# Summing rows of 1,024: each partition owns 113 consecutive rows, and the lead tile is no longer transposed

## The chip, the cores and the metric

The kernel runs on one core of one Trainium2 chip. The metric is the device time of one execution in microseconds (us).

## The reference

```python
batch, seq, dim = 32, 512, 1024
x = np.random.randn(batch, seq, dim).astype(np.float32)
multiplier = 0.5
out = (np.sum(x, axis=-1) * multiplier).astype(np.float32)
```

16,384 rows of 1,024 floats (67.1 MB) are read, and 16,384 floats (64 KB) are written.

## The kernel before

**Rows and partitions.** There are 128 partitions and 128 rows for each. The rows of x are cut into three regions, one after the other in DRAM:

- `x_rows`: the first 128 × 112 rows. Partition p owns the 112 consecutive rows from 112p on (`own = 112`), so neighbouring partitions are 112 × 4 KB = 448 KB apart.
- `x_last`: the next 128 × 15 rows (`tail = 15`), 15 consecutive rows (60 KB) for each partition.
- `x_lead`: the last 128 rows of x, one for each partition, a single stretch of 512 KB.

**Loads.** All DMAs are issued by SyncE (SP), through the helper `load` (line 83), which gives each a semaphore of its own. First comes the lead tile, then seven blocks of 16 rows per partition (8.39 MB each; 64 KB per partition in one piece) into three buffers `buf[0..2]` in turn. From the fourth block on a load waits until DVE has summed the block that held its buffer. `start_loads_at_entry` moves the lead load and the first three block loads, which wait for nothing, to the start of the program, ahead of the common preamble. The tail's 15 rows come last, in pieces of 7, 5 and 2 rows into a block buffer, and the last row cut into 608 and 416 columns into the tile `end`. Each such tile is 128 partitions wide.

**Sums.** DVE sums the lead tile with one `dve_sum` (lines 98 to 109: one instruction adds the two halves of a row and accumulates), while block 0 is still on its way. The result is 128 sums in one column, one in each partition. It goes to column 0 of a zeroed 32×32-block tile `lead_sq`, and a DVE transpose (line 129) turns it into `lead_tr`, where partitions 0, 32, 64 and 96 hold 32 sums each. These four partitions are stored with a DMA of their own (line 171, `lead_store`).

The blocks are summed by one `reduce_sum` per block (line 134) and multiplied into `res` (line 140). In the last block DVE does 8 rows and ACT the other 8 (`act_row`, line 90). In the tail the rows of the set `on_act` go to ACT, the others to DVE by `dve_sum`. The two pieces of the last row are summed by DVE in `first` and `final`, the second adding up both.

**Stores.** The early store (line 167) writes `res[:, 0:112]`, 448 bytes from each partition, once the last block is summed; the lead store follows it on the same queue. The last store (line 195) writes the tail's 15 columns, 60 bytes from each partition, after ACT's and DVE's last sums. Then SyncE waits for the three stores in the order early, lead, last (lines 199 to 201).

Of the kernel before, what the change touches and what calls it, by code (L numbers as in the profile page):

```python
# [9 lines left out]
def kernel(  # L10
# [13 lines left out]
    nc = tc.nc  # L24
# [4 lines left out]
    P = nc.NUM_PARTITIONS  # L29
# [3 lines left out]
    x_flat = x.flatten_outer_dims()  # L33
    N, D = x_flat.shape
    rows = N // P
    out_flat = out.rearrange("b s -> (b s)")
    mul = float(multiplier)

    B = 16
    n_blocks = rows // B  # L40
    assert N == P * rows and rows == n_blocks * B
    own = rows - B
    tail = B - 1
    lead0 = P * (own + tail)
    x_rows = x_flat[0 : P * own, :].rearrange("(p c) d -> p c d", p=P)
    x_last = x_flat[P * own : lead0, :].rearrange("(p c) d -> p c d", p=P)
    x_lead = x_flat[lead0:N, :]
    out_rows = out_flat[0 : P * own].rearrange("(p c) -> p c", p=P)
    out_last = out_flat[P * own : lead0].rearrange("(p c) -> p c", p=P)
    out_lead = out_flat[lead0:N].rearrange("(q c) -> q c", c=32)  # L50

    def sbuf(name, *shape):
        return ctx.enter_context(nc.sbuf_tensor(name, list(shape), fp32)).ap()
# [4 lines left out]
    res = sbuf("res", P, rows)  # L58
    cut = 608
    at = 640  # L60
    end = sbuf("end", P, at + D - cut)
    S = 32
    lead = sbuf("lead", P, D)
    lead_sq = sbuf("lead_sq", P, S)
    lead_tr = sbuf("lead_tr", P, S)

    def sem(name):
        return nc.alloc_semaphore(name=name)

    dve_done = sem("dve_done")  # L70
# [3 lines left out]
    def marks(i, engine):  # L74

        s = dve_done if engine == "dve" else act_done
        i.then_inc(s, 1)
        counts[engine] += 1
        return counts[engine]

    def load(name, dst, src, free=None):
        landed = sem(name)
        i = nc.sync.dma_start(out=dst, in_=src)  # L83
        if free is not None:
            i.wait_op(dve_done, free, "sem-ge")
        i.then_inc(landed, 16)
        return landed

    def act_row(t, r, col):
        return nc.scalar.activation(  # L90
            out=t[:, r, :],
            in_=t[:, r, :],
            func=mybir.ActivationFunctionType.Copy,
            scale=mul,
            accum_out=res[:, col : col + 1],
        )

    def dve_sum(row, dst, scale):
        mid = row.shape[-1] // 2
        return nc.vector.tensor_tensor_reduce(  # L100
            out=row[:, 0:mid],
            in0=row[:, 0:mid],
            in1=row[:, mid:],
            scale=scale,
            scalar=0.0,
            op0=ADD,
            op1=ADD,
            accum_out=dst,
        )

    marks(nc.vector.memset(end[:, at - 2 : at], 0.0), "dve")  # L111
    zeroed = marks(nc.vector.memset(lead_sq, 0.0), "dve")  # L112
    freed = []
    lead_landed = load("lead_landed", lead, x_lead)
    for b in range(n_blocks - 1):
        c0 = b * B
        t = buf[b % bufs]
        landed = load(
            f"landed{b}",
            t,  # L120
            x_rows[:, c0 : c0 + B, :],
            freed[b - bufs] if b >= bufs else None,
        )
        h = B if b < n_blocks - 2 else B // 2
        if b == 0:
            nc.vector.wait_ge(lead_landed, 16)
            nc.vector.wait_ge(dve_done, zeroed)
            summed = marks(dve_sum(lead, lead_sq[:, 0:1], mul), "dve")
            turned = nc.vector.transpose(out=lead_tr, in_=lead_sq)  # L129
            turned.wait_op(dve_done, summed, "sem-ge")  # L130
            marks(turned, "dve")
        nc.vector.wait_ge(landed, 16)
        done = marks(
            nc.vector.reduce_sum(  # L134
                out=sums[:, c0 : c0 + h], in_=t[:, 0:h, :], axis=mybir.AxisListType.X
            ),
            "dve",
        )
        freed.append(done)
        scaled = nc.vector.tensor_single_scalar(  # L140
            out=res[:, c0 : c0 + h],
            in_=sums[:, c0 : c0 + h],
            scalar=mul,
            op=mybir.AluOpType.mult,
        )
        scaled.wait_op(dve_done, done, "sem-ge")
        early_dve = marks(scaled, "dve")
        if h < B:
            nc.scalar.wait_ge(landed, 16)
            for r in range(h, B):  # L150
                i = act_row(t, r, c0 + r)
            early_act = marks(i, "act")

    c0 = (n_blocks - 1) * B
    t = buf[(n_blocks - 1) % bufs]
    nc.sync.wait_ge(dve_done, freed[n_blocks - 1 - bufs])
    pieces = [(0, 7), (7, 12), (12, 14)]
# [4 lines left out]
    landed_end = [  # L162
        load(f"landed_e{k}", end[:, to : to + hi - lo], x_last[:, tail - 1, lo:hi])
        for k, (to, lo, hi) in enumerate(((0, 0, cut), (at, cut, D)))
    ]
    nc.sync.wait_ge(dve_done, early_dve)
    early = nc.sync.dma_start(out=out_rows, in_=res[:, 0:own])
    early.wait_op(act_done, early_act, "sem-ge")
    early_stored = sem("early_stored")
    early.then_inc(early_stored, 16)  # L170
    lead_store = nc.sync.dma_start(out=out_lead, in_=lead_tr[0:P:S, :])
    lead_stored = sem("lead_stored")
    lead_store.then_inc(lead_stored, 16)

    on_act = {4, 5, 6, 10, 11, 13}
    for k, (lo, hi) in enumerate(pieces):
        on = [r for r in range(lo, hi) if r in on_act]
        nc.scalar.wait_ge(landed[k], 16)
        for r in on:
            i = act_row(t, r, c0 + r)  # L180
        late_act = marks(i, "act") if k == len(pieces) - 1 else None
        on = [r for r in range(lo, hi) if r not in on_act]
        nc.vector.wait_ge(landed[k], 16)
        for r in on:
            dve_sum(t[:, r, :], res[:, c0 + r : c0 + r + 1], mul)
    nc.vector.wait_ge(landed_end[0], 16)
    first = dve_sum(end[:, 0:cut], end[:, at - 1 : at], 1.0)

    first.then_inc(landed_end[1], 1)
    final = dve_sum(end[:, at - 2 :], res[:, rows - 2 : rows - 1], mul)  # L190
    final.wait_op(landed_end[1], 17, "sem-ge")
    done = marks(final, "dve")

    nc.sync.wait_ge(act_done, late_act)
    store = nc.sync.dma_start(out=out_last, in_=res[:, own : own + tail])
    store.wait_op(dve_done, done, "sem-ge")
    stored = sem("stored")
    store.then_inc(stored, 16)
    nc.sync.wait_ge(early_stored, 16)
    nc.sync.wait_ge(lead_stored, 16)  # L200
    nc.sync.wait_ge(stored, 16)

    def start_loads_at_entry(nc_):
# [61 lines left out]
```

## Time and profile before

| what | value |
|---|---|
| median of 3 runs | 160.57 us (160.52 to 160.6) |
| profiled execution, its own time | 160.62 us |
| its span, first to last instruction | 159.3 us |
| DVE busy | 120.2 us (75%) |
| ACT busy | 16.3 us (10%) |
| HBM read, written | 67.11 MB, 0.07 MB |
| mean DMA rate over the span | 422 GB/s |
| lead load, issue to landing | 3.2 us |
| early store, last store, issue to landing | 9.6 us, 1.4 us |

Times in the profile count from the first instruction of the span. A group of instructions is named by its line, engine, operation and tiles; L83 is line 83 of the kernel, where all loads are issued, and SPq is SyncE's instruction queue. In a timeline line the first number is the start, the second the duration, and the bracket the engine's idle time just before and what ended it. In a line of waits the numbers are the total, the count and the longest. The line of a DMA queue gives packets, MB and the packets' time as a share of sixteen DMA engines' span. TensorE is not used.

### The profile page before, as it was taken

Reading aid. Unit: us, or ns where it says so; the run is one execution under the profiler, and the core shown is the slowest. Engines: PE = TensorE matmul, PEld = TensorE weight load, DVE = VectorE, ACT = ScalarE, POOL = GpSimd, SP = SyncE. Lnnn points to the kernel's source line nnn. Section 1 sums busy time; section 2 is a strip of 40 time slices with the busy share of each in tenths; the row PEclk is TensorE's granted clock in tenths of the full one; section 3 lists DMA queues with packets and bytes.
Section 4 is the critical chain, followed back from the end, with each engine's and each line's share of the span. In section 5 each row is a group of like instructions: output and inputs, shape, how many; then the busy total and the mean of one; then the engine's idle time right before and its main releaser. Section 6 shows DMA issues by size and latency. Waiting matters only on the chain.

```text
span 159.3 us, 128 instructions
## 1 busy us (share of the span) xinstructions
DVE 120.2 (75%) x39; ACT 16.3 (10%) x29; POOL 0.2 (0%) x4
## 2 busy tenths in 40 slices
DVE  2000029999499995999869997899959999599744
ACT  2000000000000000000000000000000000099844
POOL 0000000000000000000000000000000000000000
DMA  9969989899699699699699898996996996999994
GB/s 395 510 280 527 411 379 527 379 411 527 263 527 527 263 527 527 263 527 494 296 527 428 362 527 379 411 527 280 510 527 263 527 527 263 436 403 433 442 397 144
DMA packets 2168, 67.18 MB, mean 422 GB/s; under 512 B 504, under 2 KB 632, under 8 KB 888
## 3 DMA queue, kind: packets, MB, share of 16 engines
q1 hardware_dynamic: 2168, 67.18, 98.0%
HBM read 67.11 MB, written 0.07 MB: 422 GB/s over the span
## 4 chain that ended last, share of the span: by engine, by line
DMA 75%; DVE 22%; SPq 1%; issue 0%
DMA xb<-in_x_dram 52%; DMA end<-in_x_dram 24%; DVE sums L134 22%; SPq L83 1%; DVE end L100 1%; DVE res L140 0%; DVE res L100 0%
## 5 line engine op out<-in xcount | busy, mean ns | idle before, releaser
L134 DVE TENSOR_REDUCE sums<-xb 128x16 f32<-128x16384 f32 (+1 forms) x7 | 112.0, 16001 | 30.3 <-DMA xb<-in_x_dram 30.3
L90 ACT ACTIVATE xb<-xb 128x1024 f32<-128x1024 f32 x14 | 14.6, 1046 | 138.1 <-DMA xb<-in_x_dram 138.0
L100 DVE CUSTOM_DVE_ANT_0 xb<-xb 128x512 f32<-128x512 f32 x8 | 5.1, 689 | 3.9 <-DMA xb<-in_x_dram 3.9
L90 ACT ACTIVATION_READ_ACCUMULATOR xb<-xb 128x1 f32 x14 | 2.6, 188 | 0.0
L111 DVE MEMSET end<- 128x2 f32 x1 | 0.1, 60 | 2.9 <-PEq L26 2.9
L90 ACT ACT_TABLE_LOAD x1 | 1.3, 1283 | 2.9 <-PEq L26 2.9
L140 DVE TENSOR_SCALAR res<-sums 128x16 f32<-128x16 f32 (+1 forms) x7 | 1.2, 174 | 0.2
L100 DVE CUSTOM_DVE_ANT_0 end<-end 128x304 f32<-128x304 f32 (+1 forms) x2 | 0.9, 428 | 0.1
L100 DVE CUSTOM_DVE_ANT_0 lead<-lead 128x512 f32<-128x512 f32 x1 | 0.7, 693 | 0.2 <-DMA lead<-in_x_dram 0.2
L100 DVE DVE_READ_ACCUMULATOR2_ANT res<- 128x1 f32 x9 | 0.8, 83 | 0.0
L129 DVE STREAM_TRANSPOSE lead_tr<-lead_sq 128x32 f32<-128x32 f32 x1 | 0.2, 211 | 0.0
L246 POOL MEMSET const-bfloat16-1.0<- 128x1 bf16 x1 | 0.1, 101 | 0.0
L246 POOL MEMSET const-uint8-127<- 128x1 uint8 x1 | 0.1, 101 | 0.0
L246 POOL MEMSET const-float32-0.0<- 128x1 f32 x1 | 0.1, 98 | 0.2 <-issue 0.2
L246 POOL MEMSET const-float32-1.0<- 128x1 f32 x1 | 0.1, 98 | 0.0
L112 DVE MEMSET lead_sq<- 128x32 f32 x1 | 0.1, 85 | 0.0
L100 DVE DVE_READ_ACCUMULATOR2_ANT end<- 128x1 f32 x1 | 0.1, 84 | 0.0
L100 DVE DVE_READ_ACCUMULATOR2_ANT lead_sq<- 128x1 f32 x1 | 0.1, 83 | 0.0
## 6 DMA issues: line engine op xcount, KB each, us to landing
xb<-in_x_dram SPq DMA_DIRECT2D x1, 3584.0 KB, 29.9
xb<-in_x_dram SPq DMA_DIRECT2D x1, 2560.0 KB, 35.7
xb<-in_x_dram SPq DMA_DIRECT2D x1, 1024.0 KB, 37.7
lead<-in_x_dram SPq DMA_DIRECT2D x1, 512.0 KB, 3.2
end<-in_x_dram SPq DMA_DIRECT2D x1, 304.0 KB, 37.9
end<-in_x_dram SPq DMA_DIRECT2D x1, 208.0 KB, 38.0
xb<-in_x_dram SPq DMA_DIRECT2D x7, 40.8
out_dram<-res SPq DMA_DIRECT2D x1, 56.0 KB, 9.6
```

The lines of the kernel that those rows point to most:

```text
L83: i = nc.sync.dma_start(out=dst, in_=src)
L90: return nc.scalar.activation(out=t[:, r, :], in_=t[:, r, :], func=mybir.ActivationFunctionType.Copy, scale=mul, accum_out=res[:, col : co ...
L100: return nc.vector.tensor_tensor_reduce(out=row[:, 0:mid], in0=row[:, 0:mid], in1=row[:, mid:], scale=scale, scalar=0.0, op0=ADD, op1=ADD, ...
L111: marks(nc.vector.memset(end[:, at - 2 : at], 0.0), "dve")
L112: zeroed = marks(nc.vector.memset(lead_sq, 0.0), "dve")
L129: turned = nc.vector.transpose(out=lead_tr, in_=lead_sq)
L134: nc.vector.reduce_sum(out=sums[:, c0 : c0 + h], in_=t[:, 0:h, :], axis=mybir.AxisListType.X),
L140: scaled = nc.vector.tensor_single_scalar(out=res[:, c0 : c0 + h], in_=sums[:, c0 : c0 + h], scalar=mul, op=mybir.AluOpType.mult,)
L246: nc = _bacc.Bacc("TRN2", target_bir_lowering=False, num_devices=1)
```

## The change

Partition p now owns the 113 consecutive rows from 113p on (`first = 113`), so neighbouring partitions are 452 KB apart. The lead tile is the last of these 113 rows (column `own = 112`): 128 rows of 4 KB, 452 KB apart. Its sums go straight to column 112 of `res`; the tile `lead_sq`, its memset, the transpose, `lead_tr`, the lead store and the wait for it are gone. The early store writes `res[:, 0:113]`, 452 bytes from each partition. The tail's 15 rows for each partition now lie at the end of x, and their sums in columns 113 to 127 of `res`.

```diff
-    lead0 = P * (own + tail)
-    x_rows = x_flat[0 : P * own, :].rearrange("(p c) d -> p c d", p=P)
-    x_last = x_flat[P * own : lead0, :].rearrange("(p c) d -> p c d", p=P)
-    x_lead = x_flat[lead0:N, :]
-    out_rows = out_flat[0 : P * own].rearrange("(p c) -> p c", p=P)
-    out_last = out_flat[P * own : lead0].rearrange("(p c) -> p c", p=P)
-    out_lead = out_flat[lead0:N].rearrange("(q c) -> q c", c=32)
+    first = rows - tail
+    x_rows = x_flat[0 : P * first, :].rearrange("(p c) d -> p c d", p=P)
+    x_last = x_flat[P * first : N, :].rearrange("(p c) d -> p c d", p=P)
+    out_rows = out_flat[0 : P * first].rearrange("(p c) -> p c", p=P)
+    out_last = out_flat[P * first : N].rearrange("(p c) -> p c", p=P)
...
-    zeroed = marks(nc.vector.memset(lead_sq, 0.0), "dve")
     freed = []
-    lead_landed = load("lead_landed", lead, x_lead)
+    lead_landed = load("lead_landed", lead, x_rows[:, own, :])
...
             nc.vector.wait_ge(lead_landed, 16)
-            nc.vector.wait_ge(dve_done, zeroed)
-            summed = marks(dve_sum(lead, lead_sq[:, 0:1], mul), "dve")
-            turned = nc.vector.transpose(out=lead_tr, in_=lead_sq)
-            turned.wait_op(dve_done, summed, "sem-ge")
-            marks(turned, "dve")
+            marks(dve_sum(lead, res[:, own : own + 1], mul), "dve")
...
-    early = nc.sync.dma_start(out=out_rows, in_=res[:, 0:own])
+    early = nc.sync.dma_start(out=out_rows, in_=res[:, 0:first])
...
-    lead_store = nc.sync.dma_start(out=out_lead, in_=lead_tr[0:P:S, :])
-    lead_stored = sem("lead_stored")
-    lead_store.then_inc(lead_stored, 16)
...
-    store = nc.sync.dma_start(out=out_last, in_=res[:, own : own + tail])
+    store = nc.sync.dma_start(out=out_last, in_=res[:, first:rows])
...
-    nc.sync.wait_ge(lead_stored, 16)
```

What else differs is naming: the columns of the tail are counted from `first` instead of `c0`, and the sum of the first end piece is called `part`.

More of the change, by code (lines that the diff above doesn't have):

```diff
@@ L61 @@
     end = sbuf("end", P, at + D - cut)
-    S = 32
     lead = sbuf("lead", P, D)
-    lead_sq = sbuf("lead_sq", P, S)
-    lead_tr = sbuf("lead_tr", P, S)
     def sem(name):
@@ L152 @@
             early_act = marks(i, "act")
-    c0 = (n_blocks - 1) * B
     t = buf[(n_blocks - 1) % bufs]
@@ L179 @@
         for r in on:
-            i = act_row(t, r, c0 + r)
+            i = act_row(t, r, first + r)
         late_act = marks(i, "act") if k == len(pieces) - 1 else None
@@ L184 @@
         for r in on:
-            dve_sum(t[:, r, :], res[:, c0 + r : c0 + r + 1], mul)
+            dve_sum(t[:, r, :], res[:, first + r : first + r + 1], mul)
     nc.vector.wait_ge(landed_end[0], 16)
-    first = dve_sum(end[:, 0:cut], end[:, at - 1 : at], 1.0)
-    first.then_inc(landed_end[1], 1)
-    final = dve_sum(end[:, at - 2 :], res[:, rows - 2 : rows - 1], mul)
+    part = dve_sum(end[:, 0:cut], end[:, at - 1 : at], 1.0)
+    part.then_inc(landed_end[1], 1)
+    final = dve_sum(end[:, at - 2 :], res[:, rows - 1 : rows], mul)
     final.wait_op(landed_end[1], 17, "sem-ge")
```

## Prediction

> **What bounds the kernel now.** I read the page's busy shares first, then the chain that ended last, the timeline and SyncE's waits, and at last the trace's records of single DMA packets and of the sixteen engines' completions. The page gives the bound.
>
> ```profile
> DVE 120.2 (75%) x39; ACT 16.3 (10%) x29; POOL 0.2 (0%) x4
> ...
> q1 hardware_dynamic: 2168, 67.18, 98.0%
> ...
> DMA 75%; DVE 22%; SPq 1%; issue 0%
> ```
>
> The packets of the single queue take 98.0% of sixteen engines' span, so there is nothing to win by overlapping more. DVE's 22% in the chain is not a bound either: the chain walks through a load that waited for a buffer, while two other loads were still queued. The timeline shows it.
>
> ```profile
> 22.81 17.22 DVE L134 TENSOR_REDUCE sums<-xb 128x16 f32<-128x16384 f32 x1 [18.62 <-DMA xb<-in_x_dram]
> ...
> 42.25 17.22 DVE L134 TENSOR_REDUCE sums<-xb 128x16 f32<-128x16384 f32 x1 [2.01 <-DMA xb<-in_x_dram]
> ...
> 61.61 17.22 DVE L134 TENSOR_REDUCE sums<-xb 128x16 f32<-128x16384 f32 x1 [1.93 <-DMA xb<-in_x_dram]
> ```
>
> Each reduction starts when its block lands, and waits about 1.9 us for it. Blocks land 61.61 − 42.25 = 19.36 us apart, whereas DVE needs 17.22 + 0.17. Of 8.39 MB per block that is 433 GB/s. In the packet records a block is 128 packets of 65,536 bytes, eight per engine, and most take exactly 2.418 us, which is also the shortest; 8 × 2.418 = 19.34. Each engine runs at its floor of 27.1 GB/s. Between the landings of block 1 (42.23) and block 6 (138.99) the latest engine moves 40 packets in 96.76 us, 2.419 us each: no stall worth speaking of.
>
> So the time is: when the stream gets going, plus bytes over a fixed rate, plus what follows the last landing. The end of the timeline:
>
> ```profile
> 156.87 0.48 DVE L100 CUSTOM_DVE_ANT_0 end<-end 128x304 f32<-128x304 f32 x1
> ...
> 157.39 0.38 DVE L100 CUSTOM_DVE_ANT_0 end<-end 128x209 f32<-128x209 f32 x1
> ...
> 157.80 0.35 SPq L195 DMA_DIRECT2D out_dram<-res  x1
> ```
>
> The second end tile is complete at 157.37 by its sixteen completions (the first engine is done at 156.87), the sum of it starts 0.02 us later, and the last store follows; it lands at 159.24 and the span ends at 159.28. From the last landing to the end is 1.91 us. The spread between first and last engine is 0.40 us at block 0's landing (22.39 to 22.79) and still 0.50 at the end: what the slowest engine loses in the first microseconds it carries to the end unchanged. That loss is the one thing that this change can reach.
>
> How large is it? The lead tile's 128 packets of 4,096 bytes take 0.159 us at best and 0.187 on average: 8 × 0.028 = 0.22 us per engine. Block 0's first sixteen large packets are on average 0.141 us over the floor (the worst 0.390), the next three rounds 0.027, later ones near zero; with 0.016 for the last four, about 0.24. Together 0.46 us per engine.
>
> **The change, part by part.** The profiled execution took 160.62 us: span 159.28 and 1.34 around it; the median of the three runs is 160.57. I sum against 160.62.
>
> *DVE.* One memset (0.085 us) and the transpose (0.211) go. They lie between 2.9 and 4.2 us, ahead of the 18.62 us wait for block 0. Worth 0; DVE could be 18 us later there before anything felt it. The wait of the reduction queue for the lead tile stays, with the same cover.
>
> *SyncE.* The lead store's issue (0.62 us at 148.39) and one wait go. The queue's own waits show where that lies:
>
> ```profile
> SPq L194 <- ACT xb L90: 8.3, 1, 8.3
> SPq L201 <- DMA out_dram<-res: 1.0, 1, 1.0
> SPq L195 <- DVE res L100: 0.5, 1, 0.5
> ```
>
> After the lead store SyncE waits 8.3 us for ACT, then 0.5 for DVE; no load is queued behind it, the last having been issued by 119.8. Worth 0. The removed wait, too, stands ahead of the wait for the last store; the lead store's completions end at 157.49, the last store's at 159.24.
>
> *The lead store's packets.* Four packets of 0.013 us on four engines, started at 156.6 to 156.8, after those engines' loads. The last store's packets start only at 158.65. Worth 0.
>
> *The early store* grows from 448 to 452 bytes per partition, and its rows in DRAM no longer start at multiples of 64 bytes. Now a packet takes 0.025 us, eight per engine, from 156.41 on, behind the loads of the same queue, so no load waits for it. It lands 9.6 us after its issue, at 157.6. No row shows 452 bytes. By size it is 0.025 × 452/448, a gain of nothing and a loss of nothing; were each packet to take four times as long, 8 × 0.075 = 0.6 us would be added after 157.1, still ended by 157.7, ahead of 158.65. The last store's 60-byte rows, just as unaligned, take 0.008 to 0.011 us each, so I take 0.
>
> *The tail's rows* move by 512 KB of DRAM, with the same 60 KB from partition to partition, the same pieces and shapes. Worth 0; ACT's and DVE's shares of the tail stay.
>
> *The lead load* is where a real price hides. Now its 512 KB are one stretch; then they are 128 rows of 4 KB, each 452 KB from the next. Bytes, packets and the 0.39 us issue stay. No row shows 4 KB rows at such a distance. From below: all its present excess goes, −0.22 us. From above: each packet pays what a block's first packet pays on average, 8 × 0.141 = +1.13. Nearest are small rows at a distance in the tail: 8,192 bytes take 0.309 at best and 0.312 on average, 2,432 bytes 0.098, 1,664 bytes 0.069, with 60 KB between rows. That is the floor rate plus 0.007 to 0.008 us, as the lead's 0.159 is: a jump costs nothing in a running stream. Jumps of 448 KB cost nothing either from block 0's fifth round on. I take 0.
>
> *Block 0's start.* Partitions lie 452 KB apart instead of 448, for every block. Nothing in this trace has that distance. The rows with 448 and 60 KB between partitions reach 26.8 to 27.1 GB/s per engine in packets of 20 KB and more. From below, block 0's excess of 0.24 us goes; from above, it doubles. I take 0.
>
> The sum is 160.62 + 0 = 160.62 for an execution like the profiled one, and at the median 160.57.
>
> The Trainium skill (DMA: Bandwidth & Descriptors, Latency and other measured facts) says that rows a large power of two apart lose bandwidth, that a few KiB of padding restore it, and recommends contiguous tiles otherwise. Padded is what a partition's pitch becomes here, from 448 to 452 KB; by that rule block 0 gains if 448 KB is near enough to the bad case. The trace disagrees for the running stream: 2.418 us is the floor at 448 KB already.
>
> **Rivals.**
>
> *The scattered lead load stalls (slower).* Place: the first two microseconds, where all engines start at once on cold rows. For it: at that very place the large packets lose 0.141 us, and four lead packets already take over 0.5. Against: only the first round suffers, so it may be the common start and not the jump. If each lead packet paid the mean of block 0's first four rounds, 0.055 us, eight cost 0.44: 161.0; with 0.141 each, 161.7. It decides from 0.04 us per packet on (8 × 0.04 = 0.32). Chance 0.16.
>
> *The start evens out (faster).* Wider spread over DRAM takes away the excess in lead and block 0. Fully, −0.46: 160.1. For it: the excess exists and is largest where sixteen engines start abreast, all on rows a multiple of 448 KB apart. Against: seven tenths of it must vanish on the slowest engine to show, and the lead load, whose rows lie closest together now, gets no nearer to the best case. It is the padding rule of the Trainium skill (the page and section above) in the only place left to it. Chance 0.15.
>
> *The new distance costs in the running stream (slower).* If every round lost 0.027 us, as block 0's second to fourth do, 56 rounds make +1.5: 162.1. Against: two other distances run at the floor. Chance 0.06.
>
> **How the numbers follow.** A difference under 0.2%, 0.32 us, is about what this kernel's measurement can't tell from none: same is 160.25 to 160.89. The forecast, no term large enough to show, has 0.63, and its own range is 160.3 to 160.85. Faster is the second rival, 0.15; slower the first and third, 0.22. The range runs from 160.1, the faster rival in full, to 161.1, just past the first price of the scattered lead; left out are its dear half and the third rival, about 0.14.
>
> **What would show it.** Right: the lead tile lands within 0.3 us of 3.2; reductions start at 22.8 and then every 19.36 us; the last store is issued within 0.3 us of 157.80. Scattered lead: it lands at 3.7 or later, and every reduction is later by the same. Even start: the first reduction before 22.5. Costly distance: more than 19.4 us between reductions. The forecast is wrong if the issue of the last store moves by over 0.32 us, or if the early store's landing, now 157.6, passes 159 and holds the end.

## Result: slower by a quarter of a per cent

The changed kernel takes 160.92 us (median of 21 runs, 160.75 to 161.43) against 160.55 (160.43 to 160.75) in the same comparison: a ratio of 1.0025, 95% interval 1.0018 to 1.0031. That is 0.37 us more, just past the 0.32 up to which I had called it no change. (160.92 lies inside my range of 160.1 to 161.1, but only because that range reached up to the first rival's price.) The profiled execution took 160.94 us: span 159.63 and 1.31 around it.

The page of the changed kernel, busy shares, queue and chain:

```profile
DVE 119.9 (75%) x37; ACT 16.3 (10%) x29; POOL 0.2 (0%) x4
...
q1 hardware_dynamic: 2160, 67.18, 97.9%
...
DMA 75%; DVE 22%; SPq 1%; issue 0%
```

The bound is the same. DVE has lost its 0.3 us of memset and transpose, the queue eight packets (the lead store's four and their completions), and none of it shows in the time. Its timeline, with start and duration in front:

```profile
3.81 0.69 DVE L95 CUSTOM_DVE_ANT_0 lead<-lead 128x512 f32<-128x512 f32 x1 [0.81 <-DMA lead<-in_x_dram]
...
23.16 17.22 DVE L124 TENSOR_REDUCE sums<-xb 128x16 f32<-128x16384 f32 x1 [18.65 <-DMA xb<-in_x_dram]
...
42.51 17.22 DVE L124 TENSOR_REDUCE sums<-xb 128x16 f32<-128x16384 f32 x1 [1.93 <-DMA xb<-in_x_dram]
...
61.88 17.22 DVE L124 TENSOR_REDUCE sums<-xb 128x16 f32<-128x16384 f32 x1 [1.93 <-DMA xb<-in_x_dram]
...
157.16 0.48 DVE L95 CUSTOM_DVE_ANT_0 end<-end 128x304 f32<-128x304 f32 x1
...
157.68 0.38 DVE L95 CUSTOM_DVE_ANT_0 end<-end 128x209 f32<-128x209 f32 x1
...
158.10 0.34 SPq L181 DMA_DIRECT2D out_dram<-res  x1
```

In the kernel before, the lead tile's sum stood here:

```profile
3.25 0.69 DVE L100 CUSTOM_DVE_ANT_0 lead<-lead 128x512 f32<-128x512 f32 x1 [0.18 <-DMA lead<-in_x_dram]
```

Now it starts at 3.81 instead of 3.25, block 0's reduction 0.35 us later than before, and the blocks then follow every 19.35 to 19.37 us. So the stream lost its time before block 0 was complete and kept the delay: the end tiles' sums start 0.29 us late and the last store is issued 0.30 late. Of the span's 0.35 us, 0.28 is the last landing of the end tile (157.65 for 157.37). The rest lies behind it: from that landing to the end of the span it is 1.98 us, before 1.91. SyncE's own waits (its last store is line 181 now, its wait for it line 186) point to where:

```profile
SPq L180 <- ACT xb L85: 8.9, 1, 8.9
SPq L186 <- DMA out_dram<-res: 1.1, 1, 1.1
SPq L181 <- DVE res L95: 0.5, 1, 0.5
```

The wait for the last store is 1.1 instead of 1.0. In the completions of its sixteen engines the last one comes 0.45 us after its last packet has started, before 0.39.

The records of packets and completions show what the first part is. Per engine, the lead's eight packets lose 0.63 us against their floor (0.22 before), and block 0's loss falls from 0.24 to 0.005. On the mean over engines that adds 0.18, but block 0 is complete on the first engine at 22.43 (22.39 before) and on the last at 23.13 (22.79 before). The spread has grown from 0.40 to 0.71 us, and a block counts as landed when its slowest engine is done.

### The profile page after: what moved, and what is told of

Same layout as the page of the kernel before. It is cut to its first block, busy times and chain, and to the rows that moved or that the text cites. A ratio compares the mean times of both kernels' runs of the same rounds, so it can differ in the third digit from the quotient of the medians.

```text
span 159.6 us, 123 instructions
## 1 busy us (share of the span) xinstructions
DVE 119.9 (75%) x37; ACT 16.3 (10%) x29; POOL 0.2 (0%) x4
## 4 chain that ended last, share of the span: by engine, by line
DMA 75%; DVE 22%; SPq 1%; issue 0%
DMA xb<-in_x_dram 52%; DMA end<-in_x_dram 24%; DVE sums L124 22%; SPq L78 1%; DVE end L95 1%; DVE res L130 0%; DVE res L95 0%
```

## Experiments

Five questions, 16 runs, one of them the changed kernel once more. Each ratio is to the kernel before in the same comparison, on the same chip, where its median is 160.54 to 160.61 us; the ratio can differ by up to 0.0010 from the quotient of the medians. For each profile I give two numbers from the records: when block 0 was complete on the last engine (B0), and how long after its last packet's start the last store was complete (LS). In the kernel before they are 22.79 and 0.39, in the changed kernel 23.13 and 0.45.

**Which part of the change costs?** Contiguous lead in the changed kernel:

```diff
-    lead_landed = load("lead_landed", lead, x_rows[:, own, :])
+    lead_landed = load("lead_landed", lead, x_flat[N - P : N, :])
```

> The changed kernel, but its lead tile is loaded from one contiguous stretch, the last 128 rows of x (so row 112 of each partition is left out and other rows stand in its column). Blocks stay 452 KB apart. Theory S (the lead's 128 scattered 4 KB rows stall at the start, which the slowest engine carries to the end): back to the kernel before, 160.5 to 160.65 us, lead landing at 3.2 us, lead packets 0.187 us on average. Theory P (the 452 KB between partitions is what costs): stays at 160.85 to 161.0. Theory M (the start costs what it costs, and the first packets on fresh rows pay it, whichever they are): block 0's first sixteen packets again 0.1 us or more over the floor of 2.418; under P's rival reading, that 452 KB removes the excess of block 0, they stay within 0.01 of the floor.

160.80 us, ratio 1.0019 (1.0010 to 1.0028); B0 22.93, LS 0.50. Between the two theories, so both were short. Block 0's first packets again lose 0.106 us: as M said, 452 KB does not remove it. With a contiguous lead 0.26 us of the loss is left, clear of zero, and in the profile 0.14 of it lies behind the end tile's landing (2.05 us from there to the end, before 1.91).

Scattered lead in the kernel before:

```diff
-    lead_landed = load("lead_landed", lead, x_lead)
+    lead_landed = load("lead_landed", lead, x_rows[:, own - 1, :])
```

> The kernel before, but its lead tile is row 111 of each partition: 128 rows of 4 KB, 448 KB apart (so the last 128 rows of x are left out). Transpose and lead store stay. Theory S: slower like the changed kernel, 160.85 to 161.0 us, lead landing at 3.7 us or later, spread between first and last engine about 0.7 us, block 0's packets at the floor since the lead has paid. Theory P: 160.5 to 160.65, as before.

160.58 us, ratio 1.0003 (0.9994 to 1.0012). Theory S, by then my favourite, fell here. The lead packets do lose more, 0.43 us per engine, and block 0 less, 0.07, as S says. But the loss is even over the engines: the lead's completions lie 0.33 us apart, and B0 is 22.82. The timeline of this kernel:

```profile
3.34 0.69 DVE L100 CUSTOM_DVE_ANT_0 lead<-lead 128x512 f32<-128x512 f32 x1 [0.28 <-DMA lead<-in_x_dram]
...
22.84 17.22 DVE L134 TENSOR_REDUCE sums<-xb 128x16 f32<-128x16384 f32 x1 [18.55 <-DMA xb<-in_x_dram]
```

The lead's sum starts only 0.09 us later than before, and block 0's 0.03.

Lead behind block 0, in the changed kernel:

```diff
-    lead_landed = load("lead_landed", lead, x_rows[:, own, :])
     for b in range(n_blocks - 1):
...
+        if b == 0:
+            lead_landed = load("lead_landed", lead, x_rows[:, own, :])
...
```

> The changed kernel with the scattered lead load issued behind block 0 instead of ahead of it, and its sum on DVE moved behind block 0's reduction; everything is computed. Theory S in the form that a jump costs at the cold start alone: lead packets at 0.159 us, their floor, and block 0's first packets now pay the start, some 0.14 to 0.4 us each, once per engine; total 160.4 to 160.7 us, faster than the changed kernel by 0.2 to 0.5. If small scattered packets cost wherever they stand: no change, 160.9, with lead packets at 0.2 us or more in mid-stream. Theory P: 160.9.

161.04 us, ratio 1.0041 (1.0028 to 1.0055); LS 0.45. Block 0, now first, was complete on the last engine at 21.77, the lead tile behind it at 22.99. A miss on the time, right on the packets: all 128 lead packets took 0.159, so a jump of 452 KB is free in the running stream. But now block 0's first sixteen packets lose 0.634 us each, as much as lead and block 0 together in the changed kernel (0.638). Starting cold is what costs, and it costs no less when large packets come first. (Large packets 448 KB apart were not put first in any run.) Its profile (160.78) is the lowest of its five runs and shows no more than that.

Without transpose and lead store, loads as before:

```diff
-            turned = nc.vector.transpose(out=lead_tr, in_=lead_sq)
...
-    lead_store = nc.sync.dma_start(out=out_lead, in_=lead_tr[0:P:S, :])
...
```

> The kernel before without the zeroing of lead_sq, the transpose, the lead store and the wait for it (the last 128 results are not written). The lead load stays contiguous, blocks 448 KB apart. All theories: 160.45 to 160.65 us, no difference that shows, since all that is left out lies beside the stream. A move of more than 0.1 us would say that my zeros for these parts are wrong.

160.59 us, ratio 1.0007 (0.9998 to 1.0016); B0 22.81, LS 0.39. The zeros stand.

**Loads or stores?** From the kernel without the lead store, the changed stores alone, and the changed place of the last store alone:

```diff
-    out_rows = out_flat[0 : P * own].rearrange("(p c) -> p c", p=P)
-    out_last = out_flat[P * own : lead0].rearrange("(p c) -> p c", p=P)
+    out_rows = out_flat[0 : P * (own + 1)].rearrange("(p c) -> p c", p=P)
+    out_last = out_flat[P * (own + 1) : N].rearrange("(p c) -> p c", p=P)
...
```

> The loads of the kernel before (448 KB between partitions, one stretch for the lead tile), with the changed kernel's two stores: 452 bytes and then 60 bytes from each partition at the changed places (the results stand in other places than asked for, and nothing is transposed). Theory W (the stores cost: behind 452-byte rows that start at no multiple of 64 bytes the last store is complete later): 160.7 to 160.85 us, 0.15 to 0.25 over the kernel without the lead store, 160.59, and the last store's completion 0.45 to 0.50 us after its last packet has started instead of 0.39. Theory L (only the loads cost): 160.5 to 160.65, completion at 0.39.

160.71 us, ratio 1.0007 (0.9997 to 1.0016); LS 0.39 in its profile, which took 160.53, the lowest of its runs. In the range of theory W by the median, against it by the profile.

> The kernel before without transpose and lead store, its last store placed 512 bytes further on in the output, where the changed kernel has it (some results stand elsewhere or are missing). The early store stays at 448 bytes from each partition. Theory W by the early store's rows: 160.55 to 160.65, completion 0.39 us after the last packet's start. Theory W by the last store's place: 160.7 to 160.85, completion at 0.45 to 0.50. Theory L: as the first.

(Of the diff above, only the change of `out_last`.) 160.65 us, ratio 1.0003 (0.9994 to 1.0011); LS 0.46 with 448-byte rows in the early store. The completion is that of the theory of the last store's place, the time is not. So where completion is late, the 452-byte rows are not needed for it.

From the changed kernel, the old stores; and these with a contiguous lead as well:

```diff
-    out_rows = out_flat[0 : P * first].rearrange("(p c) -> p c", p=P)
-    out_last = out_flat[P * first : N].rearrange("(p c) -> p c", p=P)
+    out_rows = out_flat[0 : P * own].rearrange("(p c) -> p c", p=P)
+    out_last = out_flat[P * own : P * (own + tail)].rearrange("(p c) -> p c", p=P)
...
-    early = nc.sync.dma_start(out=out_rows, in_=res[:, 0:first])
+    early = nc.sync.dma_start(out=out_rows, in_=res[:, 0:own])
```

> The changed kernel's loads (452 KB between partitions, scattered lead), with the stores of the kernel before without the lead store: 448 bytes and 60 bytes at the old places (some results stand elsewhere or are missing). Theory W alone: 160.55 to 160.65 us. Theory L alone: 160.9, the whole loss. Both, added: 160.7 to 160.8, the last store complete 0.39 us after its last packet's start and block 0 landing later than 22.8.

160.78 us, ratio 1.0009 (1.0000 to 1.0018); B0 23.00, LS 0.39. The loads alone cost some 0.15 us of the 0.37. That the stores cost the rest is a difference taken between chips and not shown: alone, two runs back, they cost about 0.1, not told from zero.

> As the one before, but with the lead tile loaded from one stretch: of the change only the 452 KB between the partitions of the blocks is left (results in other places, row 112 of each partition left out). If the pitch costs at the start: 160.65 to 160.75 us. If it needs the scattered lead to cost, or costs nothing: 160.5 to 160.62, so that the 0.26 of the kernel with one stretch for the lead and 452 KB came from the stores.

160.66 us, ratio 1.0002 (0.9993 to 1.0010); B0 22.91, LS 0.39. On the time nothing that can be told from zero. With the changed stores the same loads took 160.80 (the first run above); the two lose 0.26 and 0.06 us, and the difference, taken between two chips, points to the stores.

**Does the lead's own distance matter, or the blocks'?** Both times the lead's rows get the other distance:

```diff
-    lead_landed = load("lead_landed", lead, x_lead)
+    lead_landed = load("lead_landed", lead, x_flat[0 : P * (own + 1), :].rearrange("(p c) d -> p c d", p=P)[:, own, :])
```

> The kernel before without transpose and lead store, its lead tile loaded from 128 rows 452 KB apart, while the blocks stay 448 KB apart (so other rows than asked for are summed into the lead's column). Theory D (a cold start of 4 KB rows 452 KB apart is uneven, whatever follows): 160.75 to 160.9 us, first and last engine of the lead 0.6 us or more apart, block 0 complete at 23.0 or later. Theory I (it needs blocks that follow at the same 452 KB): 160.5 to 160.65, spread 0.3 to 0.5.

160.66 us, ratio 1.0002 (0.9993 to 1.0010); B0 22.70, the earliest of all with the lead first. Theory D falls.

```diff
-    lead_landed = load("lead_landed", lead, x_rows[:, own, :])
+    lead_landed = load("lead_landed", lead, x_flat[0 : P * own, :].rearrange("(p c) d -> p c d", p=P)[:, own - 1, :])
```

> The kernel with the changed loads and the old stores, but with the lead's rows 448 KB apart and the blocks 452 KB (other rows than asked for are summed into the lead's column). Theory D: 160.6 to 160.68 us, as with a contiguous lead at that pitch, spread of the lead 0.3 to 0.5 us. Theory I, if it is any mixture of scattered lead and 452 KB blocks: 160.75 to 160.85, spread 0.6 or more.

160.67 us, ratio 1.0001 (0.9992 to 1.0009); lead completions 0.80 us apart, B0 23.03. The time lies in theory D's range, the profile (160.78) in theory I's:

```profile
3.74 0.69 DVE L95 CUSTOM_DVE_ANT_0 lead<-lead 128x512 f32<-128x512 f32 x1 [0.75 <-DMA lead<-in_x_dram]
...
23.06 17.22 DVE L128 TENSOR_REDUCE sums<-xb 128x16 f32<-128x16384 f32 x1 [18.62 <-DMA xb<-in_x_dram]
```

The lead and block 0 arrive as late as with the lead at 452 KB. By the profiles it is the mixture: a scattered lead, at either distance, with blocks 452 KB apart behind it. This run's median does not show it (0.08 us more than before, not told from zero). Over all profiles with the lead first B0 sorts without overlap, by 0.03 us between the second and third row; the spread sets the last row apart more plainly:

| blocks | lead | profiles | B0, us | first to last engine at B0, us |
|---|---|---|---|---|
| 448 KB | contiguous | 8 | 22.77 to 22.88 | 0.40 to 0.55 |
| 448 KB | scattered | 2 | 22.70, 22.82 | 0.46, 0.43 |
| 452 KB | contiguous | 2 | 22.91, 22.93 | 0.43, 0.53 |
| 452 KB | scattered | 5 | 23.00 to 23.21 | 0.67 to 0.71 |

(Profiles of the runs below are counted in; the kernel with the lead behind block 0 is left out.)

**Is it the last store's place?** The two stores in exchanged places, with 448-byte rows and with 452-byte rows in the early store:

```diff
-    out_rows = out_flat[0 : P * own].rearrange("(p c) -> p c", p=P)
-    out_last = out_flat[P * own : lead0].rearrange("(p c) -> p c", p=P)
+    out_rows = out_flat[P * tail : lead0].rearrange("(p c) -> p c", p=P)
+    out_last = out_flat[0 : P * tail].rearrange("(p c) -> p c", p=P)
...
```

> The kernel before without transpose and lead store, with its two stores in exchanged places: the last store's 60-byte rows at the start of the output, the early store's 448-byte rows behind them (results in other places). Theory A (rows of 452 bytes in the early store delay the last store's completion): 160.5 to 160.65 us, completion 0.39 us after the last packet's start. Theory B (the last store's place decides): anything from 160.5 to 160.8, and the same as in the next kernel.

160.59 us, ratio 0.9998 (0.9989 to 1.0006), LS 0.39.

> As the one before, with 452-byte rows in the early store and 113 columns (results in other places). Theory A: 0.1 us or more over the kernel with 448-byte rows and completion at 0.45 to 0.50 us. Theory B: within 0.05 us of it, with the same time of completion.

160.57 us, ratio 0.9995 (0.9986 to 1.0003), LS 0.39. No difference: the unaligned 452-byte rows cost nothing.

```diff
-    out_rows = out_flat[0 : P * own].rearrange("(p c) -> p c", p=P)
-    out_last = out_flat[P * own : lead0].rearrange("(p c) -> p c", p=P)
+    out_rows = out_flat[P * (tail + 1) : N].rearrange("(p c) -> p c", p=P)
+    out_last = out_flat[P : P * (tail + 1)].rearrange("(p c) -> p c", p=P)
...
```

> The kernel before without transpose and lead store, its last store 512 bytes past the start of the output, the early store at 8,192 bytes (results in other places). If an offset of 512 bytes from a multiple of 4,096 delays the completion: 160.65 to 160.75 us and 0.45 us or more after the last packet's start. If only the end of the output does: 160.5 to 160.62 and 0.39.

160.60 us, ratio 0.9999 (0.9990 to 1.0007), LS 0.39. The offset of 512 bytes is not it.

The whole changed computation with the tail's rows first, beside the changed kernel once more, on one chip:

```diff
-    x_rows = x_flat[0 : P * first, :].rearrange("(p c) d -> p c d", p=P)
-    x_last = x_flat[P * first : N, :].rearrange("(p c) d -> p c d", p=P)
-    out_rows = out_flat[0 : P * first].rearrange("(p c) -> p c", p=P)
-    out_last = out_flat[P * first : N].rearrange("(p c) -> p c", p=P)
+    x_rows = x_flat[P * tail : N, :].rearrange("(p c) d -> p c d", p=P)
+    x_last = x_flat[0 : P * tail, :].rearrange("(p c) d -> p c d", p=P)
+    out_rows = out_flat[P * tail : N].rearrange("(p c) -> p c", p=P)
+    out_last = out_flat[0 : P * tail].rearrange("(p c) -> p c", p=P)
```

> The changed kernel with its two regions exchanged: the tail's 15 rows for each partition lie at the start of x, the 113 rows behind them, so that the last store writes the first 7,680 bytes of the output. Everything is computed. Theory B (the place of the last store costs 0.1 to 0.2 us, the loads the rest): 160.72 to 160.82 us, completion 0.39 us after the last packet's start, and 0.1 to 0.2 less than the changed kernel beside it. If the place costs nothing: as the changed kernel, 160.85 to 161.0.

160.75 us, ratio 1.0009 (1.0000 to 1.0017); B0 23.03, LS 0.39.

> The changed kernel as it is, for a second profile on the chip of the other runs of this group: 160.85 to 161.0 us, first and last engine of the lead 0.6 us or more apart, block 0 complete at 23.0 or later, the last store complete 0.45 us or more after its last packet's start.

161.12 us, ratio 1.0031 (1.0019 to 1.0043); B0 23.21, LS 0.61. That is above the expected range, and 0.37 us over the kernel with the tail first, where I had expected 0.1 to 0.2; the two intervals do not overlap. SyncE's wait for the last store, of the changed kernel again:

```profile
SPq L186 <- DMA out_dram<-res: 1.3, 1, 1.3
```

and with the tail first:

```profile
SPq L186 <- DMA out_dram<-res: 1.1, 1, 1.1
```

From the end tile's last landing to the end of the span it is 2.15 us in the one and 1.91 in the other. That is 0.24 of the 0.41 us between their spans; the rest lies ahead of that landing (157.69 against 157.51), since block 0 too was 0.18 later. Completions of the last store come about 0.008 us apart; at the end of the output one or two gaps of 0.09 to 0.15 us stand among them, in five of six profiles; elsewhere, in eleven profiles, none is over 0.032 (the last kernel below not counted).

**What the transpose was good for.** The kernel before without it, the lead's sums stored as they stand:

```diff
-    out_lead = out_flat[lead0:N].rearrange("(q c) -> q c", c=32)
+    out_lead = out_flat[lead0:N].rearrange("(p c) -> p c", p=P)
...
-    lead_store = nc.sync.dma_start(out=out_lead, in_=lead_tr[0:P:S, :])
+    lead_store = nc.sync.dma_start(out=out_lead, in_=res[:, rows - 1 : rows])
```

> The kernel before without the transpose: the lead's sums go to the last column of the results and are stored straight from it, 4 bytes from each of 128 partitions, behind the early store; everything is computed. Loads as before. All theories: 160.5 to 160.65 us, since 128 small packets (at 0.011 us each as the last store's, eight per engine, 0.09 us) lie between the early store's end at 157.1 and the last store's start at 158.6.

165.50 us, ratio 1.0299 (1.0275 to 1.0323), a clear miss. The three stores (early, lead, last) in this kernel, KB and us from issue to landing:

```profile
out_dram<-res SPq DMA_DIRECT2D x1, 56.0 KB, 16.0
out_dram<-res SPq DMA_DIRECT2D x1, 0.5 KB, 15.8
out_dram<-res SPq DMA_DIRECT2D x1, 7.5 KB, 6.5
```

and in the kernel before (the view gives no landing for the lead store; its last completion is at 157.49):

```profile
out_dram<-res SPq DMA_DIRECT2D x1, 56.0 KB, 9.6
out_dram<-lead_tr SPq DMA_DIRECT2D x1, 0.5 KB
out_dram<-res SPq DMA_DIRECT2D x1, 7.5 KB, 1.4
```

The 128 packets of 4 bytes take 0.009 us each in the records, about what I had reckoned (0.011), and are all started by 157.02. But the store's completions trickle in until 164.06, 7.0 us after the last start, which is 0.055 us for each of the 128 rows if they are shared out evenly, and those of the early and the last store on the same engines come late with them (the last at 164.23). The packet's time is not the write's time.

## Why the prediction was wrong

**Right, with their numbers.** DVE's memset and transpose, SyncE's issue, the removed wait and the lead store's packets are worth nothing (160.59 without them). The early store's 452 bytes are worth nothing: the pair with exchanged places differs by 0.02 us. The running stream does not care for 452 KB: 19.35 to 19.37 us per block. The third rival is out.

**The step that failed: lead load and block 0's start, both taken at 0.** I priced them as a mean over engines, and there the sum was not far off: +0.18 us in the profile. The time follows the slowest engine, which lost 0.34 at block 0, the spread going from 0.40 to 0.71. Both zeros rested on rows from the running stream. These rows were right (behind block 0 the scattered lead's packets took 0.159 us), but the change falls on the first packets, and for these the trace before had no row at the new distances. My own sentence that the slowest engine's loss is carried to the end should have made me price the spread; it holds nearly as it stands. In 15 of the 17 profiles with the lead first, the end tile landed 134.45 to 134.52 us after block 0. The profile before is one of the two others: there the slowest engine lost another 0.08 us between blocks 0 and 1 (134.58 in all), so that the 0.34 at block 0 became 0.28 at the end. In runs the two together cost 0.14 to 0.18 us (loads alone 160.78 against 160.60, tail first 160.75 against 160.61), with intervals that reach down to zero; with the lead's rows 448 KB apart they cost 0.08.

**The first rival had the place and not the mechanism.** Its packets paid 0.079 us over the floor instead of 0.028, past its point of 0.04, and the lead landed at 3.78, past its sign of 3.7. But the reductions came 0.35 us later and not 0.56, as the lead did; and that its 161.0 came near is luck in part, for the loads alone gave 160.78. Scattered rows alone don't make a slow kernel (160.58 at 448 KB); by the profiles they do so only with blocks 452 KB apart behind them. I had treated the two distances as separate terms.

**The second rival did not happen.** Block 0's excess did vanish, but the lead's grew by more: 0.64 us together, before 0.46. The padding rule of the Trainium skill (DMA: Bandwidth & Descriptors, Latency and other measured facts) says that a few KiB of padding restore what a pitch of a large power of two loses. At 448 KB the running stream had nothing to restore, and no run here gained by the padding: with the lead first, block 0 was complete at 22.91 us or later in every profile with 452 KB, at 22.88 or earlier in every one with 448.

**A term was missing: the last store's place.** I costed the tail's rows in x and the early store's rows, and never the last store, which moves 512 bytes and so to the end of the output. Behind the last landing it costs 0.07 and 0.24 us in the two profiles of the changed kernel. Moving the tail's rows to the front took 0.37 off on one chip, but in the profiles part of that lies ahead of the last landing. Before the change, 0.85 of the last store's 1.43 us from issue to landing pass before its first packet starts, and 0.39 after its last one has started; only this second part grew. The Trainium skill (DMA: Bandwidth & Descriptors, Anatomy of one DMA, there for DMAs that GpSimd issues) puts most of a DMA's fixed time into the receipt of the write. This trace does not agree for SyncE's store: what follows the last packet's start is the smaller part.

**What stays open.** Measured one by one, the parts give 0.05 to 0.11 us for the place and 0.14 to 0.18 for the loads, 0.19 to 0.29 together; the whole change is 0.37, and 0.51 on another chip. Taken off instead of put on, the changed stores are worth more: 0.19 us with the scattered lead (0.37 against 0.18) and 0.20 with the contiguous one (0.26 against 0.06), each between two chips. The intervals (about 0.14 us to each side) allow the sum, and do not show it. Why blocks 452 KB apart make a scattered lead uneven, and why the end of the output is written late, no run told. No version here beats the kernel before; of those that compute everything with 113 rows per partition, the one with the tail first is the best, 0.14 us behind it.

## What to carry to other kernels

In a kernel whose DMA queue is never empty, look at the completions of each engine and price a change by the slowest: what it loses in the first microseconds is still missing at the end. A new layout moves the stores too; the last store's write has nothing to hide behind, so its place belongs in the sum. And a small transpose that keeps a store's rows long can be worth far more than it costs: here it cost nothing that showed and saved 4.9 us.

## What the runs showed of the hardware

- 128 rows of 4 bytes, side by side in DRAM and written by all engines, took 7.0 us to complete, though their packets took 0.009 us each; the kernel lost 4.9 us. Stored as four rows of 128 bytes, the same 512 bytes were complete at 157.49, ahead of the early store.
- The first packets of the program's loads lose time whatever they are: 0.30 to 0.72 us per engine over lead and block 0, and 0.64 with block 0 first. Mid-stream, 4 KB rows 452 KB apart run at their floor of 0.159 us.
- The last store's completion was later at the end of the output (0.45 to 0.61 us after its last packet's start in five of six profiles) than at the three other places (0.39 in all eleven profiles).
